# Sums carried on in the matmul banks in the seven-product jobs of a decoder block

## The chip, the cores and the metric

The kernel runs on one core of a Trainium2 chip. Its engines are named here as the profile names them: TensorE (PE) multiplies matrices into PSUM, which this kernel uses as eight banks of 128 partitions by 512 float32; VectorE (DVE) and ScalarE (ACT) do elementwise work and read and write PSUM and SBUF; GpSimd (POOL) and SyncE (SP) mostly issue transfers. The metric is the device time of one execution in microseconds (us); less is better.

## The reference

One layer of a decoder block, float32, 1024 tokens of 1024 features:

```python
proj = rms_norm(x) @ w_in       # stick-breaking q, k, v | gated-linear q, k, v, output gate r, code a | two gates
o_sb  = stick_breaking_attention(sb_q, sb_k, sb_v)                      # 8 heads of 64
log_a = log_sigmoid(g_a @ w_alpha_up + b_alpha) / 16
o_gla = norm_per_head(gla_chunked(g_q, g_k, g_v, log_a)) * gla_norm_g * silu(g_r)
y = sigmoid(gate_sb + b0) * (o_sb @ w_branch_sb) + sigmoid(gate_gla + b1) * (o_gla @ w_branch_gla)
h = x + y @ w_out
a, g = split(rms_norm(h) @ w_ffn_in)                                    # 2816 features each
h = h + (gelu(causal_conv3(a)) * g) @ w_ffn_out
return rms_norm(h)
```

The change lies in two of these products: a part of `@ w_in`, and `@ w_ffn_in`.

## The kernel before

**Precision.** Every operand is cut into a high and a low part: `split` lets ScalarE cast the high part (L119) and VectorE subtract it from the source for the low part (L110). A product over 512 contraction rows, `mac` (L195), is 4 contraction tiles by 3 matmuls (high by high, high by low, low by high), twelve matmuls of 128x128 by 128x512 into one bank.

**A job.** `fast` computes two blocks of 128 output features for all 1024 tokens at once. It treats them as a 2x2 block product and does it in seven products of quarters instead of eight (Strassen, in Winograd's form). The weight quarters b11, b12, b21, b22 of a job, and their sums s1 to s4, are cut by `piece` into w11, w1, w2, w3, w4, w21 and w22; the tokens' quarters 11, 12, 22 and their sums s1 to s4 lie ready in `q`. Each product gets a bank of its own, in the order w11, w2, w3, w4, w1, w21, w22. ScalarE copies the first into c (L280). VectorE then adds up (all L116): u = w2 + c, g = w3 + u, the upper half of o1 = w4 + g, g = w1 + g, u = w1 + u, the lower half of o1 = w21 + c, u = w22 + u. u and g are the two halves of o2. While a job's products run, the next job's weights are loaded (L171) and cut: `first_pieces` (w11, w2) behind the fourth product, `more_pieces` (w3, w4, w1) behind the last; w21 and w22 are cut in their own job.

**Where it runs.** Ten jobs are projections, `@ w_in` (from about 113 to 311 us in the trace): two for the gated-linear queries and keys, four for the stick-breaking ones, two for the output gate r, two for branch gates. Numbered 0 to 9, jobs 1, 3, 5 and 7 have steps of `decayed` between them and their forerunner: two matmuls on TensorE (L467) and, on ScalarE, L468, L469, L470 and L471, of which the last two load another table of functions first (ACT_TABLE_LOAD); L501 and L502 are the transposes of an earlier step and their copy. The output gates' jobs, 6 and 7, end with a sigmoid of 128x1024 on both results (L513), the branch gates' with L516. Twenty-two jobs are `@ w_ffn_in` (about 834 to 1230 us): each ends with the convolution `ff_out`, begun by ScalarE (L996), carried on by VectorE (L998 twice), then gelu (L1000) and a multiplication (L113). Six of the twenty-two have two of their products done earlier (`done` is set); sixteen have all seven in the job.

**Behind the projections** the attention begins: `qk` loads queries and keys of a pair of heads (L573, L574, L567, L571, SP's queue), casts them (L578, L581), subtracts (L110, 64x1024), and `weigh` multiplies them (L631, L632), with sigmoids L634 and L635 behind. Between them stand products of the remaining gates (`gates`, L195). Behind the feed-forward jobs stands the output stage (L1098).

**Order.** A scheduler puts each engine's instructions into one fixed order when the kernel is built; on the chip each engine runs its list in that order and waits where an operand or a buffer is not ready. SBUF tiles come from rings of 8, 4 and 2 KB (`t8`, `t4`, `t2`); a new tile waits for the last users of the slot it is given.

## Time and profile before

| what | value |
|---|---|
| time, median of 3 runs | 1451.14 us (1451.05 to 1451.71) |
| span of the profiled execution | 1448.6 us |
| TensorE busy | 1428.3 us (99%), 6569 matmuls |
| VectorE busy | 1102.5 us (76%) |
| ScalarE busy | 682.1 us (47%) |
| GpSimd busy | 152.9 us (11%) |
| matmuls of L195 | 3648, 869.8 us |
| share of L195 in the chain that ended last | 56% |

The span runs from the first to the last instruction of one profiled execution; the times of the runs are taken without the profile and hold some microseconds around it. Busy time is the sum of an engine's instructions. The chain that ended last is followed back from the last instruction, at each step to what released it.

### The profile page before, as it was taken

The page shows a single profiled execution, that of the slowest core. Times are in us where ns is not written, and L with a number is a line of the kernel's source. Part 1 is how long each engine was busy: PE and PEld are TensorE (multiplying, and loading weights), DVE is VectorE, ACT ScalarE, POOL GpSimd, SP SyncE. Part 2 cuts the span into 40 slices and gives each one's busy share as a digit, 9 for nine tenths or more (in the row PEclk, how much of TensorE's full clock was granted, in tenths as well). Part 3 has the DMA queues.
Part 4 walks back from the last instruction along what each step waited for, and adds up shares of the span by engine and source line. Part 5 has one row for each costly group of instructions (what it writes and reads, how often), then busy time and mean ns, then how long its engine had stood idle before and what let it go on. Part 6 is the DMA issues. An engine that isn't in the chain of part 4 may idle for free.

```text
span 1448.6 us, 18651 instructions
## 1 busy us (share of the span) xinstructions
PE 1428.3 (99%) x6569; PEld 1154.1 (80%) x6569; DVE 1102.5 (76%) x1737; ACT 682.1 (47%) x1310; POOL 152.9 (11%) x277
## 2 busy tenths in 40 slices
PE   7999999999999999999999999999999999999997
PEld 6788888877777778878888888888888888888886
DVE  6397667868988976735834999898888887897855
ACT  6225444647867665452322643343333333554554
POOL 0000000022442431300000000010000000000000
PEclk9999999999999999999999999999999999999999
DMA  6332342467525415637332622755534436963332
GB/s 243 127 107 73 109 123 89 138 218 206 129 77 138 124 47 174 215 104 243 125 131 87 175 73 93 242 177 179 168 126 162 164 116 232 339 199 102 96 102 102
DMA packets 156798, 212.67 MB, mean 147 GB/s; under 512 B 9713, under 2 KB 102963, under 8 KB 156192
## 3 DMA queue, kind: packets, MB, share of 16 engines
q1 hardware_dynamic: 138096, 155.44, 35.4%
q0 software_dynamic: 11312, 41.48, 7.5%
q10 hardware_dynamic: 7296, 14.55, 2.7%
q8 instruction: 52, 0.85, 0.2%
q14 instruction: 42, 0.34, 0.1%
HBM read 153.64 MB, written 57.80 MB: 146 GB/s over the span
## 4 chain that ended last, share of the span: by engine, by line
PE 94%; DVE 3%; DMA 1%; ACT 1%; issue 1%; SPq 0%; DVEq 0%; ACTq 0%
PE bank L195 56%; PE bank L1098 14%; PE bank L366 6%; PE bank L965 5%; PE bank L663 2%; PE bank L654 2%; PE bank L632 2%; DVE t L110 2%; PE bank L631 1%; PE bank L319 1%; PE bank L794 1%; PE bank L789 1%; DVE t L116 1%; PE bank L774 1%; DMA t<-sqk_d 1%
## 5 line engine op out<-in xcount | busy, mean ns | idle before, releaser
L195 PE MATMUL bank<-t,t 128*128 128x512 f32 x3648 | 869.8, 394 | 0.8 <-DVE t L110 0.8
L195 PEld LDWEIGHTS bank<-t,t 128*128 128x128 f32 x3648 | 677.5, 188 | 155.6 <-issue 10.2
L110 DVE TENSOR_TENSOR t<-t,t 128x512 fp32r<-128x512 f32 (+1 forms) x659 | 439.3, 699 | 90.5 <-ACT t L119 81.0
L119 ACT CAST t<-t 128x512 fp32r<-128x512 f32 x537 | 311.3, 619 | 296.2 <-DVE t L110 68.4
L116 DVE TENSOR_TENSOR t<-bank,t 128x512 f32<-128x512 f32 (+1 forms) x284 | 182.9, 654 | 116.5 <-PE bank L195 67.1
L1098 PE MATMUL bank<-t,t 128*128 128x512 f32 x924 | 209.6, 389 | 0.0
L1098 PEld LDWEIGHTS bank<-t,t 128*128 128x128 f32 x924 | 173.4, 188 | 36.0
L113 DVE TENSOR_TENSOR t<-t,t 128x511 f32<-128x511 f32 (+5 forms) x134 | 92.8, 697 | 2.1 <-ACT t L513 0.8
L366 PE MATMUL bank<-t,t 128*128 128x512 f32 x384 | 90.8, 395 | 0.0
L965 PE MATMUL bank<-t,t 128*128 128x512 f32 x384 | 88.9, 391 | 0.0
L110 DVE TENSOR_TENSOR t<-bank,t 128x512 fp32r<-128x512 f32 (+4 forms) x128 | 72.5, 576 | 19.7 <-ACT t L119 19.4
L996 ACT ACTIVATE t<-t,vcol 128x1024 f32<-128x1024 f32 x22 | 27.4, 1245 | 127.4 <-DVE t L116 127.4
L366 PEld LDWEIGHTS bank<-t,t 128*128 128x128 f32 x384 | 72.0, 189 | 15.4 <-DVE t L110 0.4
L965 PEld LDWEIGHTS bank<-t,t 128*128 128x128 f32 x384 | 71.7, 188 | 14.6
L116 DVE TENSOR_TENSOR t<-t,t 128x512 f32<-128x512 f32 x107 | 70.2, 687 | 16.1 <-ACT t L471 15.3
L110 DVE TENSOR_TENSOR t<-t 128x512 f32<-128x512 f32 x116 | 78.5, 685 | 4.1 <-DMA t<-in_w_ffn_in_dram 3.7
L119 ACT CAST t<-bank 128x512 fp32r<-128x512 f32 (+3 forms) x124 | 61.7, 512 | 38.6 <-PE bank L319 19.0
L638 POOL TENSOR_SCALAR_AFFINE_SELECT t<-t 128x128 f32<-128x128 f32 x128 | 66.2, 535 | 123.3 <-ACT t L634 118.2
L998 DVE SCALAR_TENSOR_TENSOR t<-t,vcol,t 128x1023 f32<-128x1023 f32 (+1 forms) x44 | 56.3, 1278 | 14.1 <-ACT t L996 13.9
L646 DVE TENSOR_TENSOR_SCAN t<-t,zero 128x128 f32<-128x128 f32 (+1 forms) x64 | 52.3, 821 | 15.9 <-POOL t L638 15.7
L634 ACT ACTIVATE t<-bank 128x128 f32<-128x128 f32 (+3 forms) x96 | 48.2, 502 | 17.2 <-PE bank L632 15.0
L654 PE MATMUL bank<-ident,t 128*128 128x128 f32 x288 | 49.7, 278 | 1.7 <-DVE t L113 0.9
(125 smaller groups left out, 891.1 us busy)
## 6 DMA issues: line engine op xcount, KB each, us to landing
t<-in_w_ffn_in_dram SPq DMA_DIRECT2D x50, 512.0 KB, 5.0
t<-in_w_in_dram SPq DMA_DIRECT2D x43, 512.0 KB, 5.3
act_d<-t POOLq DMA_DIRECT2D x22, 512.0 KB, 5.8
t<-in_w_ffn_out_dram SPq DMA_DIRECT2D x22, 512.0 KB, 6.5
wsum_d<-t POOLq DMA_DIRECT2D x22, 512.0 KB, 4.6
t<-act_d SPq DMA_DIRECT2D x22, 512.0 KB, 5.8
t<-wsum_d SPq DMA_DIRECT2D x44, 256.0 KB, 3.2
t<-sqk_d SPq DMA_DIRECT2D x40, 256.0 KB, 5.7
```

Of the source, the lines that this page charges most:

```text
L110: nc.vector.tensor_tensor(out=o, in0=a, in1=b, op=ALU.subtract)
L113: nc.vector.tensor_tensor(out=o, in0=a, in1=b, op=ALU.mult)
L116: nc.vector.tensor_tensor(out=o, in0=a, in1=b, op=ALU.add)
L119: nc.scalar.copy(h, src)
L195: nc.tensor.matmul(pt, a[:, kk], b[:, kk], start=start and kk == 0 and m == 0, stop=stop and kk == k - 1 and m == 2)
L366: nc.tensor.matmul(pt, a[:, k % 4, t], b, start=k == 0 and m == 0, stop=k == NK - 1 and m == 2)
L638: nc.gpsimd.affine_select(out=a[:, w - P:w], in_=a[:, w - P:w], pattern=[[-1, P]], compare_op=ALU.is_gt, fill=fill_, base=0, channel_multi ...
L646: nc.vector.tensor_tensor_scan(out=kr, data0=kr, data1=zero.to_broadcast([P, w]), initial=initial, op0=ALU.mult, op1=ALU.add)
L654: nc.tensor.transpose(pt[:, b * P:(b + 1) * P], be[:, b * P:(b + 1) * P], ident)
L965: nc.tensor.matmul(pt, a[:, k % 4, t], b, start=(k == 0 and m == 0), stop=(k == NK - 1 and m == 2))
L998: nc.vector.scalar_tensor_tensor(out=cv[:, i:], in0=av[:, :S - i], scalar=col(V_CW, (2 - i) * NF + f), in1=cv[:, i:], op0=ALU.mult, op1=AL ...
L1098: nc.tensor.matmul(pts[m][i], a[:, t], b, start=(k == 0 and x_ == 0), stop=(k == NH - 1 and x_ == 2))
```

## The change

Jobs whose seven products are all still to do (ten projections, sixteen of feed-forward) take a new function, `whole`. It uses three banks, px, py and pz. The products run in the order w11 (px), w1 (py), w2 (onto px), w21 (pz), w3 (onto px), w22 (onto py), w4 (onto px). `mac` gets a switch `more`, with which its first matmul does not clear the bank. ScalarE copies px after w11 (c), py after w1 (g), px after w2 (u) and px after w4 (the upper half of o1); VectorE adds the lower half of o1 = pz + c, g = px + g after w3, u = py + u after w22. For these jobs w1 is cut in `first_pieces`. The six jobs with `done` set keep the old way.

```diff
-    def mac(w, r, k=4, pt=None, start=True, stop=True):
+    def mac(w, r, k=4, pt=None, start=True, stop=True, more=False):
+        start = start and not more
...
                 nc.tensor.matmul(pt, a[:, kk], b[:, kk], start=start and kk == 0 and m == 0,
-                                 stop=stop and kk == k - 1 and m == 2)
+                                 stop=stop and kk == k - 1 and m == 2, skip_group_check=more)
...
             sub(s2, b22, r["s1"])
+            if r["done"] is None:
+                r["w1"] = piece(r["s1"])
             r["w2"] = piece(s2)
...
             r["w4"] = piece(s4)
-            r["w1"] = piece(r["s1"])
+            if r["done"] is not None:
+                r["w1"] = piece(r["s1"])
+
+        def whole(r, nxt, o1, u, g):
+            px, py, pz = bank(), bank(), bank()
+            c = t2()
+            mac(r["w11"], q["11"], pt=px)
+            nc.scalar.copy(c, px)
+            w21 = piece(r["a"][:, 4:])
+            mac(r["w1"], q["s1"], pt=py)
+            nc.scalar.copy(g, py)
+            w22 = piece(r["b"][:, 4:])
+            mac(r["w2"], q["s2"], pt=px, more=True)
+            nc.scalar.copy(u, px)
+            mac(w21, q["12"], pt=pz)
+            add(o1[:, :HALF], pz, c)
+            if nxt is not None:
+                first_pieces(nxt)
+            yield
+            mac(r["w3"], q["s3"], pt=px, more=True)
+            add(g, px, g)
+            mac(w22, q["s4"], pt=py, more=True)
+            add(u, py, u)
+            if nxt is not None:
+                more_pieces(nxt)
+            mac(r["w4"], q["22"], pt=px, more=True)
+            nc.scalar.copy(o1[:, HALF:], px)
...
             if r["done"] is None:
-                c = t2()
-                nc.scalar.copy(c, mac(r["w11"], q["11"]))
-            else:
-                c = r["done"][:, :HALF]
-                nc.scalar.copy(o1[:, :HALF], r["done"][:, HALF:])
+                yield from whole(r, nxt, o1, u, g)
+                finish(o1, o2)
+                yield
+                continue
+            c = r["done"][:, :HALF]
+            nc.scalar.copy(o1[:, :HALF], r["done"][:, HALF:])
...
-                    if r["done"] is None:
-                        w21 = piece(r["a"][:, 4:])
...
-            if r["done"] is None:
-                add(o1[:, :HALF], mac(w21, q["12"]), c)
```

The lines of the changed kernel are numbered anew. In the new `fast`, L260 is the copy c, L263 g, L266 u, L279 the upper half of o1, and L198 the matmul; of the lines behind it L497 to L500 are the decays' L468 to L471, L512 and L513 their L483 and L484, L531 and L532 the L502 and L503 of before, L542 the sigmoid of L513, L1025 and L1027 the convolution's L996 and L998, and L1127 the matmul of L1098.

Three places in the order of the engines follow. ScalarE between jobs 6 and 7, before: the sigmoids of job 6's two results (L513), between them the copy of the transposes (L502).

```order
L513 ACT_TABLE_LOAD
L513 ACTIVATE t4_329_2037<-t4_308_1906 128x1024
L502 COPY t2_280_1740<-bank_331_2045 128x512
L513 ACTIVATE t4_330_2041<-t4_309_1907 128x1024
L503 DMA kt_d_83<-t2_280_1740 128x512
```

And now, from the last copy of job 6 (L279) on:

```order
L279 COPY t4_284_1876<-bank_286_1878 128x512
L531 COPY t2_260_1715<-bank_303_2010 128x512
L542 ACT_TABLE_LOAD
L542 ACTIVATE t4_301_2002<-t4_284_1876 128x1024
L542 ACTIVATE t4_302_2006<-t4_285_1877 128x1024
```

Both sigmoids now stand behind the last copy of job 6.

A little later on ScalarE, in job 7, before: the two casts for w21 and w22 (L119), the last table load of the decays ahead of c, and the copy c (L280).

```order
L119 CAST t4_341_2088<-t8_307_1903 128x512
L471 ACT_TABLE_LOAD
L471 ACTIVATE t2_332_2052<-t2_332_2052 128x512
L119 CAST t4_342_2091<-t8_307_1903 128x512
L280 COPY t2_339_2073<-bank_340_2074 128x512
```

And now, to the copy c (L260):

```order
L119 CAST t4_315_2055<-t8_283_1873 128x512
L500 ACT_TABLE_LOAD
L500 ACTIVATE t2_304_2017<-t2_304_2017 128x512
L263 COPY t4_310_2037<-bank_312_2039 128x512
L119 CAST t4_316_2071<-t8_283_1873 128x512
L260 COPY t2_314_2041<-bank_311_2038 128x512
```

The copy of the second product (L263) now stands ahead of the copy c, beside the cast for w22.

TensorE in the same job, before: the end of the first product (bank_340) and the start of the second, in a bank of its own.

```order
L195 MATMUL bank_340_2074<-t8_3_97,t4_317_1971 128x512 x2
L195 MATMUL bank_340_2074<-t8_4_98,t4_317_1971 128x512
L195 MATMUL bank_340_2074<-t8_3_97,t4_317_1971 128x512
L195 MATMUL bank_343_2094<-t8_116_714,t4_320_1978 128x512
L195 MATMUL bank_343_2094<-t8_117_715,t4_320_1978 128x512
L195 MATMUL bank_343_2094<-t8_116_714,t4_320_1978 128x512 x2
```

And now: the end of w1's product (bank_312), eight matmuls of w21's (bank_313), and the start of w2's, which goes on in the first product's bank_311 and waits for the copy c.

```order
L198 MATMUL bank_312_2039<-t8_127_797,t4_295_1947 128x512
L198 MATMUL bank_312_2039<-t8_126_796,t4_295_1947 128x512
L198 MATMUL bank_313_2040<-t8_5_99,t4_315_2055 128x512
L198 MATMUL bank_313_2040<-t8_6_100,t4_315_2055 128x512
L198 MATMUL bank_313_2040<-t8_5_99,t4_315_2055 128x512 x2
L198 MATMUL bank_313_2040<-t8_6_100,t4_315_2055 128x512
L198 MATMUL bank_313_2040<-t8_5_99,t4_315_2055 128x512 x2
L198 MATMUL bank_313_2040<-t8_6_100,t4_315_2055 128x512
L198 MATMUL bank_311_2038<-t8_116_714,t4_296_1950 128x512
L198 MATMUL bank_311_2038<-t8_117_715,t4_296_1950 128x512
```

What was a product into a fresh bank is a product onto a bank that ScalarE reads first.

VectorE at the end of the last feed-forward job, before: from its last sums to the subtractions for the output stage (the low parts of t4_1949 to t4_1952 and t4_1909, t4_1910).

```order
L116 TENSOR_TENSOR t4_1922_10708<-bank_1932_10788,t2_1924_10710 128x512
L998 SCALAR_TENSOR_TENSOR t4_1934_10816<-t4_1922_10708,vcol_75,t4_1934_10816 128x1023
L116 TENSOR_TENSOR t4_1923_10709<-bank_1933_10802,t4_1923_10709 128x512
L998 SCALAR_TENSOR_TENSOR t4_1934_10816<-t4_1922_10708,vcol_75,t4_1934_10816 128x1022
L110 TENSOR_TENSOR t4_1949_10864<-t8_1946_10858,t4_1949_10864 128x512
L110 TENSOR_TENSOR t4_1950_10867<-t2_1947_10860,t4_1950_10867 128x512
L113 TENSOR_TENSOR t4_1934_10816<-t4_1934_10816,t4_1923_10709 128x1024
L110 TENSOR_TENSOR t8_1946_10858<-t8_1946_10858 128x512
L110 TENSOR_TENSOR t4_1909_10632<-t2_1955_10905,t4_1909_10632 128x512
L110 TENSOR_TENSOR t4_1910_10635<-t8_1959_10943,t4_1910_10635 128x512
L110 TENSOR_TENSOR t4_1951_10883<-t8_1946_10858,t4_1951_10883 128x512
L110 TENSOR_TENSOR t4_1952_10886<-t2_1948_10862,t4_1952_10886 128x512
```

And now (t4_1845 to t4_1848 take the place of t4_1949 to t4_1952):

```order
L116 TENSOR_TENSOR t4_1823_10584<-bank_1824_10585,t4_1823_10584 128x512
L116 TENSOR_TENSOR t4_1823_10584<-bank_1825_10586,t4_1823_10584 128x512
L1027 SCALAR_TENSOR_TENSOR t4_1830_10686<-t4_1822_10583,vcol_75,t4_1830_10686 128x1023
L110 TENSOR_TENSOR t4_1845_10734<-t8_1842_10728,t4_1845_10734 128x512
L1027 SCALAR_TENSOR_TENSOR t4_1830_10686<-t4_1822_10583,vcol_75,t4_1830_10686 128x1022
L110 TENSOR_TENSOR t4_1846_10737<-t2_1843_10730,t4_1846_10737 128x512
L110 TENSOR_TENSOR t8_1842_10728<-t8_1842_10728 128x512
L113 TENSOR_TENSOR t4_1830_10686<-t4_1830_10686,t4_1823_10584 128x1024
L110 TENSOR_TENSOR t4_1847_10753<-t8_1842_10728,t4_1847_10753 128x512
L110 TENSOR_TENSOR t4_1848_10756<-t2_1844_10732,t4_1848_10756 128x512
L110 TENSOR_TENSOR t4_1852_10777<-t8_1849_10771,t4_1852_10777 128x512
```

The convolution's steps (L1027) come behind all three sums, and its multiplication (L113) stands ahead of the subtractions for t4_1847 and t4_1848; two subtractions that stood ahead of their likes (t4_1909, t4_1910) are behind now.

## Rows read from the trace of the kernel before

**Rows 1.** The page, part 1: busy time of each engine, share of the span, instructions.

```profile
PE 1428.3 (99%) x6569; PEld 1154.1 (80%) x6569; DVE 1102.5 (76%) x1737; ACT 682.1 (47%) x1310; POOL 152.9 (11%) x277
```

**Rows 2.** The chain in order of time: start, duration (us), what, matmuls.

```profile
834.11 396.51 PE bank L195 x1748
1230.62 209.45 PE bank L1098 x924
```

**Rows 3.** Stretches: length; busy PE, PEld, DVE, ACT, POOL (count); clock, DMA share, GB/s.

```profile
312.00:372.00 60.00, 58.71 (x277) 43.51 (x278) 52.09 (x85) 46.80 (x96) 20.75 (x36) 1.00 0.64 185
...
1002.00:1230.00 228.00, 228.00 (x1007) 188.79 (x1006) 190.60 (x275) 80.23 (x121) 12.79 (x24) 1.00 0.48 159
```

**Rows 4.** Waits of PE: line, what it waited for, us, times, longest.

```profile
PE bank L319 <- DVE t L311: 9.2, 1, 9.2
```

**Rows 5.** Instructions by line and shape: busy us, mean ns; idle before them, what ended it.

```profile
L1000 ACT ACTIVATE t<-t 128x1024 f32<-128x1024 f32 x22 | 23.4, 1062 | 40.1 <-DVE t L998 40.1
...
L280 ACT COPY t<-bank 128x512 f32<-128x512 f32 x26 | 15.0, 576 | 31.6 <-PE bank L195 31.6
...
L471 ACT ACT_TABLE_LOAD x4 | 5.1, 1283 | 0.1
```

```profile
L116 DVE TENSOR_TENSOR t<-bank,t 128x512 f32<-128x512 f32 x252 | 170.1, 686 | 106.0 <-PE bank L195 67.1 <-PE bank L965 37.0 <-PE bank L1098 1.7
```

**Rows 6.** Timeline at the start of job 1: start, duration (us), engine, instruction [idle before].

```profile
133.65 11.63 PE L195 MATMUL bank<-t,t 128*128 128x512 f32 x50
...
138.82 0.57 ACT L280 COPY t<-bank 128x512 f32<-128x512 f32 x1
```

**Rows 7.** Timeline at the start of job 7.

```profile
251.47 0.60 PE L501 MATMUL bank<-ident,t 128*128 128x128 f32 x4
...
252.11 0.59 ACT L502 COPY t<-bank 128x512 f32<-128x512 f32 x1
...
252.59 1.06 ACT L513 ACTIVATE t<-t 128x1024 f32<-128x1024 f32 x1
...
253.05 10.27 PE L195 MATMUL bank<-t,t 128*128 128x512 f32 x44
253.55 0.68 ACT L468 ACTIVATE t<-bank,vcol 128x512 f32<-128x512 f32 x1
...
256.66 0.60 ACT L119 CAST t<-t 128x512 fp32r<-128x512 f32 x1
257.28 1.28 ACT L471 ACT_TABLE_LOAD   x1
...
258.58 0.63 ACT L471 ACTIVATE t<-t 128x512 f32<-128x512 f32 x1
259.11 0.60 ACT L119 CAST t<-t 128x512 fp32r<-128x512 f32 x1
...
259.62 0.58 ACT L280 COPY t<-bank 128x512 f32<-128x512 f32 x1
```

**Rows 8.** Timeline from the last projection job to the attention.

```profile
290.06 2.66 SPq L574 DMA_DIRECT2D t<-sqk_d  x4
...
291.27 0.60 PE L501 MATMUL bank<-ident,t 128*128 128x128 f32 x4
...
296.39 6.31 SPq L171 DMA_DIRECT2D t<-in_w_in_dram  x2
...
304.73 1.14 ACT L119 CAST t<-t 128x512 fp32r<-128x512 f32 x2 [5.30 <-DMA t<-in_w_in_dram]
...
306.17 4.85 DVE L110 TENSOR_TENSOR t<-t,t 64x1024 fp32r<-64x1024 f32 x4
...
310.80 0.22 PE L631 MATMUL bank<-t,t 128*128 128x128 f32 x1
```

**Rows 9.** Timeline at the end of the feed-forward jobs.

```profile
1228.66 1.25 ACT L996 ACTIVATE t<-t,vcol 128x1024 f32<-128x1024 f32 x1 [11.96 <-DVE t L116]
```

```profile
1235.95 3.69 DVE L110 TENSOR_TENSOR t<-t,t 128x512 fp32r<-128x512 f32 x6
```

## The prediction

> **What bounds the kernel now.** I read the share of busy time first: TensorE is busy 99% of the span, VectorE 76%, ScalarE 47% [rows 1]. So a microsecond taken from VectorE is worth nothing by itself; it counts only where TensorE waits for it. The chain in time says whether it does: one piece of 396.51 us holds 1748 matmuls of the products end to end, 0.2268 us each, and the next piece, 209.45 us with 924 matmuls of the output stage, has 0.2267 [rows 2]. A product of twelve matmuls is 12 x 0.2268 = 2.72 us, and there is no room between them. By stretch: in the 228 us of steady feed-forward jobs TensorE idles for nothing while VectorE works 190.60; in the 60 us behind the projections it loses 1.29 [rows 3]. Of all 1448.6 - 1428.3 = 20.3 us of TensorE idle time [rows 1], 9.2 are one wait at the start [rows 4] and 8.5 lie behind the last matmul (1448.6 - 1230.62 - 209.45) [rows 1, 2]. **Some 2.6 us are all that any relief inside could give back.** So the question is not what VectorE saves but whether the new waits of TensorE are hidden.
>
> **What leaves and what comes.** In each of the 26 changed jobs four VectorE adds go (7 to 3) and three ScalarE copies come (1 to 4). 26 x 4 x 0.686 = 71 us of VectorE and 26 x 3 x 0.576 = 45 us of ScalarE [rows 5]; both engines have idle time, so both count nothing on the path. The 84 matmuls of a job stay. Call the products in their new order P1 to P7 (P1 w11, P2 w1, P3 w2, P4 w21, P5 w3, P6 w22, P7 w4). P3, P5 and P7 add onto P1's bank, P6 onto P2's. An add onto a bank may start only when the partial sum in it has been read: P3 waits for the copy c behind P1, P5 for the copy u behind P3, P6 for the copy g behind P2, P7 for VectorE's add behind P5. Before, every product had a bank of its own, and nothing on TensorE waited for these readers. Behind such a wait the whole TensorE queue stands, since its order is fixed.
>
> **Steady feed-forward jobs (16): nothing.** Count T from the end of the job before. ScalarE first has the copy of that job's last sum (0.58), its convolution (1.25 [rows 9]), and one weight cast (0.60), so it is free at about 2.5; P1 ends at 2.72, so c ends at 3.4 against 5.44, when P2 ends. The u copy ends 0.65 behind P3 and has P4's 2.72 us; the add behind P5 (0.686) has P6's. The gelu (1.06 [rows 5]) falls between c and g, and g has until P5's end. The cover is each time one whole other product, and the least margin about 2.0 us. If an edge of 2 us were missed, every microsecond missed would count 16 times (a rival, below).
>
> Two things move besides. The weights of w1, needed second now, are cut one step earlier, a job ahead, by the same two ScalarE casts and subtractions. And a job's convolution needs the last product now, not the sixth, so it, the gelu and the store behind it come 2.6 us later in their job; what is stored is read back only in the output stage, many jobs later, so only the last job's matters (below).
>
> **Job 1, the first decays: 0.3 us.** ScalarE does the decays and two loads of its tables ahead of c. c's copy ran at 138.82 and ended at 139.39; P1 started at 133.65, and with P2 behind it TensorE will want c at 133.65 + 2 x 2.73 = 139.11 [rows 6]. Stall 0.3 (0 to 0.6). In jobs 3 and 5 one table load fewer (1.28 [rows 5]) stands ahead of c, so 1.0 us is left over; in the others without decays there is as much room as in the steady jobs.
>
> **Job 7, decays behind two silu gates: 2.9 us.** Here ScalarE must do job 6's two sigmoids as well. Let T be 251.47, where the transposes behind job 6 start [rows 7]. Before, the first sigmoid ran ahead of T, since its sum was ready early; now its half o1 is P7's and is copied only after T, so both sigmoids come after. The copy of the transposed block starts at T + 0.64 and hands over 0.5 later; then a table load (1.3), two sigmoids (1.0 each from start to start): the decays' first step starts at T + 4.45. From there the old rows give the pace: 253.55 to the second weight cast at 259.11 is 5.56, and 0.5 from there to c [rows 7]. In the new order two steps stand ahead of c at this place, g and a cast: 4.45 + 5.56 = 10.0 for g, 10.5 for the cast, 11.1 for c, which ends at 11.7. TensorE: P1 starts at T + 1.58, P2 ends at 7.04, and the order puts eight matmuls of P4 next, to 8.86 unless they wait themselves (their operand's cast ends at 4.45 + 3.11 + 0.6 = 8.2, within the same stall). Then P3: 11.7 - 8.86 = **2.9 us** (2.3 to 3.5). Before, c came at T + 8.73, and no one on TensorE waited for it. P5's copy u is ready at 15.0, with TensorE there at 15.3: no second stall. The 2.9 us cannot be caught up later, as everything behind is bound by TensorE.
>
> The table load lasts 1.28 us at 257.28, and the next step starts 1.30 behind its start [rows 7]. The Trainium skill, page ScalarE: Activation LUTs, section on what ACT_TABLE_LOAD costs, counts a drain of 1.38 us more for each switch; with three loads ahead of c that would make job 7's stall 7.0 us, with two job 1's 3.1, and the whole some 1462. The row shows no such drain, so it decides, and the rule gets no chance of its own.
>
> **The passage to the attention: 0.8 us.** The keys' loads were issued at 290.06, 1.2 us before the last projection job began (its transposes ran at 291.27) [rows 8]. They go into an SBUF slot. Now that slot is the one of s1's low part, read last by the second product of that job: free at T + 0.6 + 2 x 2.73 = T + 6.1, 7.3 us later than before. SP's queue is held up behind it: the rest of the keys, the queries' rests and the gates' weights. Before, the last were issued from 296.39 and cast from 304.73, 8.3 us later; the first attention matmul ran at 310.80, T + 19.5, right when the job was over [rows 8]. Now the issue of the weights begins at about T + 11.4 and their cast at 20, the third of the four subtractions (4.85 in all [rows 8]) ends at about 20.1 to 20.7, where the products are over at 19.8: 0.3 to 0.9. The gate's first matmul, reached at 21.1, finds its weights between 20.9 and 23.3. Together 0 to 2.5; I take 0.8, since the row with 8.3 us to the cast is the nearest.
>
> **The passage to the output stage: 0.2 us.** The last job's convolution began at 1228.66, 2.0 us before its products ended [rows 2, 9]; now it needs the last product, so it comes at T + 0.6. VectorE's subtractions for the next stage stand behind it: the fourth of the six from 1235.95 ended at T + 7.8 [rows 9]; in the new order two of those ahead are moved behind it, and it ends at 8.5. TensorE wants it at 36 to 38 matmuls, 8.2 to 8.6. 0 to 0.8; I take 0.2.
>
> **Sum.** 0.3 + 2.9 + 0.8 + 0.2 = +4.2 us. The profiled span is 1448.6 and the median 1451.14, 2.5 above it; the difference goes on the median: **1455.3 us**.
>
> **Rivals.**
> *No change.* Job 7's c copy comes earlier than my sum of starts says, or the passages cost nothing: 1451 to 1454.0. For it: margins of under 1 us in my working, and TensorE's long pieces, which show that this order was met everywhere [rows 2]. Against it: three of the four ends would all have to fall low. Chance 0.24.
> *Faster.* With 119 fewer waits on the product line TensorE loses less between matmuls, and the 2.6 us inside shrink. At most 1451.1 - 2.6 = 1448.5, a little lower if the start-up of products that follow VectorE closely gets shorter. Against it: in the steady jobs TensorE already runs at the pace of the waitless output stage, 0.2268 to 0.2267 [rows 2]. Chance 0.06.
> *A wait in every job.* The convolution starts late in the feed-forward jobs, c slips past P2's end, and P3 waits. It decides once ScalarE frees itself later than T + 4.8. At 0.5 us for each of 16 jobs: +8, so 1463. For it: VectorE, on which the gelu hangs, works 84% of these stretches [rows 3]. Against it: c stands ahead of the gelu on ScalarE. Chance 0.07.
> The Trainium skill, page Perfetto Trace Analysis, section Matmuls, says that independent groups of matmuls should rotate through PSUM banks, so that one bank is emptied while the next group runs. With no overlap at all the 78 copies would lie bare, 45 us, and the whole come to some 1496. In this kernel another bank's product lies between in every case, 2.72 us against 0.576 [rows 2, 5], so that end belongs to the chance above and gets next to nothing of it.
> *The clock falls.* A stall of 2.9 us leaves TensorE idle, and it goes on at 1.2 instead of 2.4 GHz; a product would take 5.4 us, some 3 to 5 us more: 1459. Against it: TensorE waited 9.2 us at the start [rows 4], and the granted clock of the two stretches with and without gaps is 1.00, the higher level [rows 3]. Chance 0.03.
> My forecast, stalls in a few places, 1454.0 to 1458, has 0.60.
>
> **How the numbers follow.** A difference of 0.2%, 2.9 us, is about what a measurement of this kernel can tell from no change, so "slower" begins at 1454.0. Slower: 0.60 + 0.07 + 0.03 = 0.70; the same 0.24; faster 0.06. The range takes the likeliest case with its bounds (2.3 + 0 to 3.5 + 0.6 + 2.5 + 0.8 = 7.4) and most of the "no change" case, down to 1451.5; the rest of the slower rivals is left out: 1451.5 to 1459.
>
> **What would show it.** Waits of TensorE on the product line: one of about 3 us in job 7 (near 260 us), released by ScalarE, c's line; one of 0.3 near 139; none in the steady jobs, whose chain should be one piece at 0.2268. The keys' loads issued about 7 us later relative to the last projection job, with a wait near 315. VectorE's busy time down by 71 us and ScalarE's up by 45. I am wrong if job 7's wait is under 2 us, if TensorE waits in steady jobs, or if a matmul's mean pace in the products changes at either level of the clock.

## The result, and the profile after

The changed kernel takes 1457.83 us (median, 1457.59 to 1459.01) against 1451.10 of the kernel before on the same chip: plus 6.7 us, a ratio of 1.0048 (95% interval 1.0035 to 1.0061). The forecast was 1455.3 in 1451.5 to 1459.0, slower. The direction and the range held; 2.5 us of the loss were missed.

The page of the kernel after, part 1, to be set beside [rows 1]:

```profile
PE 1431.5 (98%) x6569; PEld 1154.4 (79%) x6569; DVE 1039.5 (71%) x1633; ACT 718.5 (49%) x1388; POOL 149.6 (10%) x277
```

VectorE did lose 104 instructions and ScalarE gained 78, as counted. TensorE does the same 6569 matmuls. What it waits for has grown; the view of its waits (line, what it waited for, us, times, longest) is to be set beside [rows 4]:

```profile
PE bank L348 <- DVE t L340: 9.0, 1, 9.0
PE bank L198 <- ACT t L260: 3.0, 2, 1.9
PE bank L198 <- ACT t L119: 1.4, 2, 0.9
...
PE bank L198 <- DVE t L110: 0.8, 1, 0.8
...
PE bank L198 <- DVE t L116: 0.4, 1, 0.4
```

In the kernel before, the product line had one wait, that ahead of the first feed-forward job:

```profile
PE bank L195 <- DVE t L110: 0.8, 1, 0.8
```

The copy c (L260) is new among the releasers, twice, with 3.0 us. The chain in order of time shows where the feed-forward one falls; of the one piece of 1748 matmuls in [rows 2] these are left:

```profile
838.37 70.12 PE bank L198 x308
909.11 7.48 DMA t<-in_w_ffn_out_dram
949.19 288.66 PE bank L198 x1272
```

From 949.19 on, 1272 matmuls run end to end at 0.2269 us, the pace of before. Between the two pieces the chain leaves TensorE for a load of w_ffn_out and for VectorE. The stretches (columns as in [rows 3]) show the place, 930 to 945 us, and that the jobs behind it are whole:

```profile
930.00:945.00 15.00, 13.06 (x58) 10.47 (x57) 15.00 (x23) 8.13 (x14) 1.59 (x3) 1.00 0.55 208
```

```profile
1010.00:1238.00 228.00, 228.00 (x1008) 188.79 (x1007) 161.98 (x226) 97.19 (x155) 12.76 (x24) 1.00 0.51 161
```

**Where the time went, stage by stage.** For every kernel I read eight marks from TensorE's timeline and its chain: the first matmul of the projections (113.62 in the kernel before), the transposes ahead of jobs 3, 7 and 9 (171.86, 251.47, 291.27), the first 24 gate matmuls in a row behind the first attention matmuls (321.16), the first feed-forward job behind its wait for VectorE (834.11), and the first and last matmul of the output stage. Lengths between marks, less those of the kernel before, in us; "elsewhere" is the rest of the span: the start, the attention and the store at the end. These differ by about 1 us from one execution to another even where the instructions are the same (the attention of ffn_only has the instructions of before in the same order and took 1.0 us longer). "Timed" is the difference of the medians. "Sum" and "elsewhere" come from one traced execution, "timed" from all: the trace of the changed kernel is that of its slowest execution, 1459.01 us.

| kernel | job 1 | jobs 7, 8 | to the attention | feed-forward | output stage | sum | elsewhere | timed |
|---|---|---|---|---|---|---|---|---|
| forecast | 0.3 | 2.9 | 0.8 | 0 | 0.2 | 4.2 | | |
| changed kernel | 0.34 | 2.92 | 0.51 | 2.97 | 0.40 | 7.1 | 1.5 | 6.7 |
| ffn_only | 0 | 0 | 0 | 2.12 | 0.37 | 2.5 | 1.2 | 3.4 |
| proj_only | 0.35 | 2.89 | 0.51 | 0.02 | 0 | 3.8 | 1.3 | 4.5 |
| tail_only | 0 | 0 | 0 | 0.01 | 0.37 | 0.4 | 0.1 | 0.4 |
| tail_copies6 | 0 | 0 | 0 | 5.10 | 0.35 | 5.5 | -0.4 | 5.5 |
| job6_old | 0.35 | 0.51 | 0.50 | 3.88 | 0.37 | 5.6 | 0.4 | 4.5 |
| three_old | 0 | 2.16 | 0.50 | 1.41 | 0.36 | 4.4 | 0.5 | 7.6 |
| from_26 | 0.35 | 2.91 | 0.51 | 0.00 | 4.55 | 8.3 | 0.2 | 8.3 |
| sums_later | 0.35 | 2.88 | 0.51 | 3.96 | 0.38 | 8.1 | 0 | 6.9 |
| no_sum_work | 0.34 | 2.92 | 0.50 | 7.62 | 0.40 | 11.8 | 0.5 | 11.9 |
| order_only | 0 | 0.41 | 0.50 | 0.28 | 0.25 | 1.4 | 0.8 | 4.2 |
| order_later | 0 | 0.43 | 2.71 | 0.14 | 0.27 | 3.6 | 1.7 | 2.4 |
| late_later | 0.25 | 1.78 | 0.49 | 2.49 | 0.25 | 5.3 | 1.5 | 6.0 |

Four of my five terms came out within 0.3 us, and they repeat in the kernels that keep the code in question; from_26 adds a loss of its own in the output stage. The feed-forward term is the one that failed.

### The profile page after: what moved, and what is told of

Read it like the earlier page. It is cut to its first block, busy times and chain, and to the rows that moved or that the text cites. A ratio compares the mean times of both kernels' runs of the same rounds, so it can differ in the third digit from the quotient of the medians.

```text
span 1457.2 us, 18493 instructions
## 1 busy us (share of the span) xinstructions
PE 1431.5 (98%) x6569; PEld 1154.4 (79%) x6569; DVE 1039.5 (71%) x1633; ACT 718.5 (49%) x1388; POOL 149.6 (10%) x277
## 4 chain that ended last, share of the span: by engine, by line
PE 90%; DVE 4%; ACT 2%; DMA 2%; issue 1%; SPq 0%; DVEq 0%; ACTq 0%
PE bank L198 52%; PE bank L1127 14%; PE bank L395 6%; PE bank L994 5%; DVE t L110 3%; PE bank L692 2%; PE bank L683 2%; PE bank L661 2%; PE bank L660 1%; DVE t L116 1%; PE bank L823 1%; PE bank L348 1%; PE bank L818 1%; PE bank L803 1%; DMA t<-sqk_d 1%
## 5 line engine op out<-in xcount | busy, mean ns | idle before, releaser
L198 PE MATMUL bank<-t,t 128*128 128x512 f32 x3648 | 872.0, 394 | 5.6 <-ACT t L260 3.0
L198 PEld LDWEIGHTS bank<-t,t 128*128 128x128 f32 x3648 | 677.0, 188 | 162.9 <-issue 9.4
L119 ACT CAST t<-t 128x512 fp32r<-128x512 f32 x537 | 308.0, 620 | 215.9 <-PE bank L1127 54.0
L1127 PE MATMUL bank<-t,t 128*128 128x512 f32 x924 | 210.0, 389 | 0.0
L1127 PEld LDWEIGHTS bank<-t,t 128*128 128x128 f32 x924 | 173.3, 188 | 36.6 <-DVE t L110 0.6
L116 DVE TENSOR_TENSOR t<-bank,t 128x512 f32<-128x512 f32 (+1 forms) x180 | 113.7, 635 | 109.3 <-PE bank L198 59.4
L113 DVE TENSOR_TENSOR t<-t,t 128x511 f32<-128x511 f32 (+5 forms) x134 | 92.5, 695 | 11.2 <-ACT t L542 9.2
L279 ACT COPY t<-bank 128x512 f32<-128x512 f32 x26 | 15.3, 587 | 171.3 <-PE bank L198 171.3
L1027 DVE SCALAR_TENSOR_TENSOR t<-t,vcol,t 128x1023 f32<-128x1023 f32 (+1 forms) x44 | 56.3, 1279 | 42.9 <-ACT t L1025 42.7
L119 ACT CAST t<-bank 128x512 fp32r<-128x512 f32 (+3 forms) x124 | 61.8, 513 | 38.6 <-PE bank L348 19.5
```

The lines of the kernel that those rows point to most:

```text
L113: nc.vector.tensor_tensor(out=o, in0=a, in1=b, op=ALU.mult)
L116: nc.vector.tensor_tensor(out=o, in0=a, in1=b, op=ALU.add)
L119: nc.scalar.copy(h, src)
L198: nc.tensor.matmul(pt, a[:, kk], b[:, kk], start=start and kk == 0 and m == 0, stop=stop and kk == k - 1 and m == 2, skip_group_check=more)
L1027: nc.vector.scalar_tensor_tensor(out=cv[:, i:], in0=av[:, :S - i], scalar=col(V_CW, (2 - i) * NF + f), in1=cv[:, i:], op0=ALU.mult, op1=AL ...
L1127: nc.tensor.matmul(pts[m][i], a[:, t], b, start=(k == 0 and x_ == 0), stop=(k == NH - 1 and x_ == 2))
```

## The experiments

**Which jobs.** A parameter of `fast` names the jobs that keep the form of before. It serves six of the runs, each with its own two lists, projections and feed-forward:

```diff
-    def fast(jobs, q, early=0):
+    def fast(jobs, q, early=0, old=()):
...
-                return dict(zip("ab", load_pair(*jobs[n][0])), done=ahead.popleft() if ahead else None)
+                r = dict(zip("ab", load_pair(*jobs[n][0])), done=ahead.popleft() if ahead else None)
+                r["carry"] = r["done"] is None and n not in old
+                return r
...
-            if r["done"] is None:
+            if r["carry"]:
                 yield from whole(r, nxt, o1, u, g)
```

The old form stands behind it as it was, and w1 is cut early only where `carry` is set.

*ffn_only* (projections: all old; feed-forward: none).

> Only the sixteen feed-forward jobs use the new form; the ten projection jobs are as before. Theory (the loss sits at a few named places: job 1 0.3 us, job 7 2.9, passage to the attention 0.5, first feed-forward job with all seven products 2.9, passage to the output stage 0.4): before plus 3.3, some 1454.4 us, with TensorE waits of 1.9 and 0.4 us near 932 and 944 us and none between 113 and 312. Rival (every job of the new form loses a little, 6.7 / 26 = 0.26 us): plus 4.1, some 1455.2, with no wait above 0.5 us.

1453.99 against 1450.63 us, ratio 1.0023 (1.0014 to 1.0032). In the trace 2.12 + 0.37 us, with TensorE's wait for c of 1.1 us at 933 us and one of 0.39 for VectorE's sum at 945, and nothing in the fifteen jobs behind.

*proj_only* (projections: none; feed-forward: all old).

> Only the ten projection jobs use the new form. Theory (named places): plus 0.3 + 2.9 + 0.5 = 3.7, some 1454.8 us, and the feed-forward stage as long as before (396.5 us in one piece). Rival (every job loses 0.26 us): plus 2.6, some 1453.7.

1455.16 us, ratio 1.0032 (1.0019 to 1.0044). The three terms of the projections repeat to 0.03 us, and the feed-forward stage is one piece of 396.52 us again. So the loss sits in places; but the two runs don't tell yet whether the steady jobs are free.

*tail_only* (projections: all old; feed-forward: the first ten old, so the new form is in the last twelve).

> The new form only in the last twelve feed-forward jobs, where VectorE has room; all else as before. Theory (steady jobs of the new form cost nothing, the passage to the output stage 0.4): 1451.2 + 0.4, some 1451.6 us, the same as before within 0.1%. Rival (each job of the new form loses 0.26 us by its waits): 12 x 0.26 = 3.1, some 1454.3.

1451.24 against 1450.86 us, ratio 1.0003 (0.9993 to 1.0012). Twelve jobs of the new form cost 0.01 us in their stage and 0.37 in the output stage. The rival of 0.26 us a job is out. The view of TensorE's waits has one on the product line, that ahead of the first feed-forward job, and none for a copy:

```profile
...
PE bank L198 <- DVE t L110: 0.8, 1, 0.8
```

The Trainium skill, page Perfetto Trace Analysis, section Matmuls, would have independent groups rotate through different banks, so that emptying one overlaps the next group's matmuls. The changed jobs carry one sum on in a bank instead, and here one other product between two on the same bank was enough in all twelve jobs. tail_only is also the answer to what the change could give: 48 VectorE sums fewer, and no time.

*tail_copies6*: the same, with the copy c made six times over.

```diff
-            nc.scalar.copy(c, px)
+            for _ in range(6):
+                nc.scalar.copy(c, px)
```

> As the run before it, but the copy c is made six times over in each of the twelve jobs (five further ScalarE copies of 0.58 us, 0.52 from start to start). Theory (c has 2.0 us to spare, and no more): the four copies that stand ahead of the gelu end at 4.9 us of the job, the sixth, behind gelu and g, at about 7.9; TensorE, which here takes some nine matmuls of the fourth product ahead, wants the bank at about 7.6: 0.3 to 0.5 us lost in each job, 4 to 6 in all, with TensorE waiting for c's line. Rival (ScalarE's copies are hidden however many, or the margin is larger): as the run before it.

1456.34 us, 5.1 above tail_only, ratio to before 1.0038 (1.0023 to 1.0052); in the trace 5.10 us in twelve jobs, 0.42 each, where 0.3 to 0.5 was worked out from the margin of 2.0 us. The timeline of one job (start, duration, engine, instruction [idle before it, and what ended that]) shows four copies, the gelu, the fifth, g, the sixth, and the wait at TensorE's weight load:

```profile
1063.71 2.45 ACT L261 COPY t<-bank 128x512 f32<-128x512 f32 x4 [0.35 <-PE bank L198]
1066.05 1.06 ACT L1040 ACTIVATE t<-t 128x1024 f32<-128x1024 f32 x1
1067.02 0.57 ACT L261 COPY t<-bank 128x512 f32<-128x512 f32 x1
1067.48 0.60 ACT L264 COPY t<-bank 128x512 f32<-128x512 f32 x1
1067.95 0.61 ACT L261 COPY t<-bank 128x512 f32<-128x512 f32 x1
...
1068.62 1.46 PEld L198 LDWEIGHTS bank<-t,t 128*128 128x128 f32 x7 [0.38 <-ACT t L261]
```

So in a steady job the copy is hidden as the hand-made timeline has it, and the cover is finite: the wait is there to be found as soon as ScalarE comes later than that.

**Job 7.** *job6_old* (projections: job 6 old; feed-forward: none).

> The changed kernel, but projection job 6 (the silu gates ahead of job 7) in the form of before, so that its first sigmoid can run ahead of job 7 again, while job 7 keeps its copy c and two table loads. Theory (job 7's wait is c standing behind two sigmoids that came late): the waits in job 7 fall from 2.9 to 0.5 us in all, 1455.4 us. Rival (the decays' table loads alone make it): it stays at 2.9, 1457.8.

1455.74 us, ratio 1.0031 (1.0020 to 1.0042). Jobs 7 and 8 lose 0.51 us instead of 2.92, as expected; the two table loads are the same. Here ScalarE's first sigmoid runs at 250.06, ahead of the transposes at 251.86, and c ends 9.2 behind these; the rows answer to [rows 7]:

```profile
250.06 1.06 ACT L552 ACTIVATE t<-t 128x1024 f32<-128x1024 f32 x1 [6.96 <-DVE t L116]
...
253.94 0.68 ACT L507 ACTIVATE t<-bank,vcol 128x512 f32<-128x512 f32 x1
...
260.49 0.59 ACT L260 COPY t<-bank 128x512 f32<-128x512 f32 x1
```

In the changed kernel the sigmoids come behind the last copy, both together, and c ends 11.6 behind the transposes (252.46):

```profile
252.66 0.58 ACT L279 COPY t<-bank 128x512 f32<-128x512 f32 x1 [7.70 <-PE bank L198]
...
255.04 2.01 ACT L542 ACTIVATE t<-t 128x1024 f32<-128x1024 f32 x2
...
256.96 0.67 ACT L497 ACTIVATE t<-bank,vcol 128x512 f32<-128x512 f32 x1
...
260.71 2.37 PE L198 MATMUL bank<-t,t 128*128 128x512 f32 x8 [0.94 <-ACT t L119]
...
263.49 0.59 ACT L260 COPY t<-bank 128x512 f32<-128x512 f32 x1
...
264.13 4.22 PE L198 MATMUL bank<-t,t 128*128 128x512 f32 x17 [1.05 <-ACT t L260]
```

I had put c's end at T + 11.7 and the decays' first step at T + 4.45; they were at 11.6 and 4.5. Both of TensorE's waits that the text named are there, for the cast of w21 and for c; 0.94 + 1.05, and the rest of the 2.92 lies inside the pieces (eight matmuls in 2.37 us, where 1.8 do). The wait itself was shared: c's line released only 1.05 us of it.

*three_old* (projections: jobs 1 and 7 old; feed-forward: the first with seven products old).

> The new form everywhere but in projection jobs 1 and 7 and in the first feed-forward job with all seven products, which keep the form of before. Theory (named places): 0.5 + 0.4 are left, some 1452.0 us. Rival (every job loses 0.26 us): 23 x 0.26 = 5.9, some 1457.0. Second rival (the feed-forward wait belongs to whichever job comes first in the new form, behind one of the old form): it turns up one job later, plus 3.8, some 1454.9.

1458.18 us (1455.29 to 1458.99), ratio 1.0047 (1.0034 to 1.0059): neither 1452 nor 1457 by its reasons. Job 1's term is gone. Job 7's is not; it moved to job 8, whose c now stands behind job 7's two sigmoids and two table loads, in ScalarE's timeline

```profile
273.75 1.28 ACT L552 ACT_TABLE_LOAD   x1
275.04 2.01 ACT L552 ACTIVATE t<-t 128x1024 f32<-128x1024 f32 x2
277.07 1.28 ACT L526 ACT_TABLE_LOAD   x1
...
278.90 0.57 ACT L260 COPY t<-bank 128x512 f32<-128x512 f32 x1
```

with a TensorE wait of 1.88 us. The feed-forward wait moved too, two jobs on, and shows its cause better than before (next). The median is 3 us above the traced execution, which was the fastest (1455.29). Its granted clock over the whole span was 0.998, that of the four other runs 0.996 or 0.997; 0.001 to 0.002 of 1455 us is some 1.5 to 3 us (an estimate), so TensorE at its lower clock is the likeliest place of the difference. Where in those runs it fell, one trace can't say.

**The feed-forward wait.** In the changed kernel it stands at the first job of the new form. TensorE wanted c at 935.68 and got it 1.94 us later; ScalarE had waited for VectorE with a cast, then did the convolution, a cast, and c:

```profile
934.81 0.62 ACT L119 CAST t<-t 128x512 fp32r<-128x512 f32 x1 [1.72 <-DVE t L110]
...
935.34 1.24 ACT L1025 ACTIVATE t<-t,vcol 128x1024 f32<-128x1024 f32 x1
936.48 0.60 ACT L119 CAST t<-t 128x512 fp32r<-128x512 f32 x1
...
936.99 0.57 ACT L260 COPY t<-bank 128x512 f32<-128x512 f32 x1
...
937.62 11.17 PE L198 MATMUL bank<-t,t 128*128 128x512 f32 x48 [1.94 <-ACT t L260]
```

VectorE is busy without a pause there (15.00 of 15 us in the stretch above). In the kernel before it was too, and c came equally late: it ended at 933.1, where the new order would have wanted it at 834.11 + 428 x 0.2268 = 931.2, 1.9 us earlier, as in the changed kernel (937.56 against 935.68). These rows of the kernel before, which I had not read, say so, and TensorE goes on at 100% beside them:

```profile
932.52 0.58 ACT L280 COPY t<-bank 128x512 f32<-128x512 f32 x1
```

```profile
915.00:930.00 15.00, 15.00 (x68) 12.43 (x67) 15.00 (x23) 5.96 (x10) 1.60 (x3) 1.00 0.61 209
930.00:945.00 15.00, 15.00 (x68) 12.43 (x67) 15.00 (x23) 5.96 (x10) 0.53 (x1) 1.00 0.50 152
```

The work that fills VectorE here beside the jobs is the sums of w_ffn_out (`weight_sums`, a step every half job from here on), whose first step also waits for its load, in the changed kernel:

```profile
916.69 2.50 DVE L110 TENSOR_TENSOR t<-t,t 128x512 f32<-128x512 f32 x4 [4.76 <-DMA t<-in_w_ffn_out_dram]
```

*sums_later*: one empty step ahead of the first subtraction.

```diff
             b11, b12, b21, b22 = a[:, :HALF], a[:, HALF:], b[:, :HALF], b[:, HALF:]
             yield
+            if k == 0:
+                yield
```

> The changed kernel, with one empty step between the first load of the weight sums (w_ffn_out) and their first subtraction on VectorE, which waited 4.8 us there at 911 us; nothing else is changed. Theory (TensorE's waits at the first feed-forward job of the new form come from that wait, passed on through VectorE's sums, ScalarE's cast and convolution to the copy c): the 1.9 and 0.4 us waits near 937 and 949 are gone, 1457.8 - 2.9 = 1454.9 us, and the runs lie closer together. Rival (the first job behind the old form waits whatever VectorE does): as the changed kernel, 1457 to 1458.

1458.14 us, ratio 1.0045 (1.0032 to 1.0058). The stage loses 3.96 us, but this doesn't settle it: VectorE still waits 3.8 us for the load at 911 us, since the scheduler placed the step hardly later, and 1.75 us for another at 950. The edit did not take away what it was to take away. It moved the loss: c came in time here (it ended at 933.6, and TensorE wanted it at 837.8 + 428 x 0.2268 = 934.9), and TensorE waited 1.99 us for a sum by VectorE at 948 instead, with the clock at the lower level behind it (last section).

*no_sum_work*: the four VectorE instructions of each step left out.

```diff
             yield
-            sub(b22, b22, b12)
-            sub(b12, b12, b11)
             yield
-            add(b11, b22, b11)
-            sub(b21, b11, b21)
```

> The changed kernel without the four VectorE subtractions and additions in each step of the sums of w_ffn_out (the rows are loaded and stored as they are, so the output stage works on other numbers); the wait for their first load goes with them. Theory (the 3 us at the first feed-forward jobs of the new form come from a VectorE that is full there, 92% busy from 834 to 1002 us, so that sums and casts that c stands behind come late): TensorE waits for nothing between 840 and 1230 us, the stage takes 396.3 us. Rival (the first job of the new form behind the old form waits in any case): the wait of 1 to 2 us near 935 stays.

1462.7 us (one run, so without an interval): against the expectation, a wait of 5.0 us for c, until 939.56. Without these instructions the scheduler put c behind the gelu in this job, and the gelu waited 3.94 us for VectorE's convolution steps. It is the rival "a wait in every job" of the prediction, at one job: c behind the gelu, and then late.

```profile
937.98 1.06 ACT L1035 ACTIVATE t<-t 128x1024 f32<-128x1024 f32 x1 [3.94 <-DVE t L1033]
938.94 0.57 ACT L260 COPY t<-bank 128x512 f32<-128x512 f32 x1
...
939.56 5.79 PE L198 MATMUL bank<-t,t 128*128 128x512 f32 x14 [4.98 <-ACT t L260]
```

The edit leaves the loads and stores of the sums in place, and they hold up the same jobs: a weight cast on ScalarE waits 6.55 us for a store, as it does in the changed kernel (6.68) and in the kernel before (6.99), and VectorE waits 4.84 us behind that cast. So the run does not separate the arithmetic of the sums from their transfers.

```profile
916.22 0.62 ACT L119 CAST t<-t 128x512 fp32r<-128x512 f32 x1 [6.55 <-DMA act_d<-t]
```

*from_26*: the steps of the sums begin eight half jobs later.

```diff
-FFN_FROM = 18
+FFN_FROM = 26
```

> The changed kernel with the weight sums' steps begun eight half jobs later (FFN_FROM 26 for 18), so that the first jobs of the new form run while VectorE has no such work. Theory (VectorE full at that place): no wait at the first job of the new form; later, with three sums a job instead of seven, VectorE has room (in the changed kernel 162 of 228 us from 1010 us on), so at most 1 us: 1457.8 - 2 to 3 = 1455 to 1456. Rival (the wait belongs to the first job of the new form): 1457 to 1458 with the wait near 935.

The feed-forward stage takes as long as in the kernel before, in one piece, though its first job of the new form follows one of the old form as ever: the rival is out, and the wait belongs to the sums that run beside these jobs, by their arithmetic or by their transfers, which moved together. The order of c and gelu alone does not make it: c stands behind the gelu in this job here too, ended at 934.1, and TensorE wanted it at 838.07 + 428 x 0.2268 = 935.1.

```profile
838.07 396.51 PE L198 MATMUL bank<-t,t 128*128 128x512 f32 x1748 [0.77 <-DVE t L110]
```

The time is 1459.16 us all the same, ratio 1.0060 (1.0046 to 1.0073): the last steps now fall into the output stage, where VectorE waits for their load and TensorE for VectorE, 2.29 us of the 4.55 lost there; most of the rest is the lower clock behind that wait (last section).

```profile
1247.21 201.35 PE L1137 MATMUL bank<-t,t 128*128 128x512 f32 x880 [2.29 <-DVE t L110]
```

three_old shows how the load of w_ffn_out can reach TensorE, there at the third job with seven products. VectorE waits 4.84 us for w_ffn_out; the convolution stands behind that, the gelu waits for it 6.06 us, g, a cast and u stand behind the gelu, and TensorE waits for u:

```profile
969.30 0.69 DVE L110 TENSOR_TENSOR t<-t,t 128x512 f32<-128x512 f32 x1 [4.84 <-DMA t<-in_w_ffn_out_dram]
...
973.89 1.27 DVE L1037 SCALAR_TENSOR_TENSOR t<-t,vcol,t 128x1022 f32<-128x1022 f32 x1
...
975.26 1.06 ACT L1039 ACTIVATE t<-t 128x1024 f32<-128x1024 f32 x1 [6.06 <-DVE t L1037]
976.22 0.57 ACT L263 COPY t<-bank 128x512 f32<-128x512 f32 x1
...
977.21 0.59 ACT L266 COPY t<-bank 128x512 f32<-128x512 f32 x1
...
977.85 1.43 PE L198 MATMUL bank<-t,t 128*128 128x512 f32 x5 [1.11 <-ACT t L266]
```

**The carry or the order.** *order_only*: the new order of products and the early cut of w1, but a bank for each product.

```diff
-            px, py, pz = bank(), bank(), bank()
             c = t2()
-            mac(r["w11"], q["11"], pt=px)
-            nc.scalar.copy(c, px)
+            nc.scalar.copy(c, mac(r["w11"], q["11"]))
...
-            mac(r["w2"], q["s2"], pt=px, more=True)
-            nc.scalar.copy(u, px)
-            mac(w21, q["12"], pt=pz)
-            add(o1[:, :HALF], pz, c)
+            add(u, mac(r["w2"], q["s2"]), c)
+            add(o1[:, :HALF], mac(w21, q["12"]), c)
+            add(c, mac(r["w3"], q["s3"]), u)
+            add(u, py, u)
...
+            add(g, c, g)
+            add(u, mac(w22, q["s4"]), u)
...
+            add(o1[:, HALF:], mac(r["w4"], q["22"]), c)
```

(c holds the sum of w11, w2 and w3 by then.)

> The new order of the products and the early cut of w1, with the copies c and g, but every product in a bank of its own again and six sums by VectorE: no matmul waits for a reader of its bank. Theory (the waits for readers make the loss): within 1 us of before, 1450.5 to 1452.0. Rival (the order, with w21 and w1 needed earlier, or the earlier cut of w1 on ScalarE and VectorE makes it): plus 4 to 7, 1455 to 1458.

1454.80 us (1452.54 to 1457.08), ratio 1.0031 (1.0019 to 1.0043); but the trace, with a span of 1450.8 us that of the fastest execution (1452.54), shows only 1.4 us in the stages: 0.41 at jobs 7 and 8, the 0.50 at the passage to the attention, 0.28 and 0.25. So at the passage to the attention the loss is the order's and not the carry's, and job 1's and most of job 7's are the carry's. How much of the feed-forward term the order alone makes stays open: the other runs lie up to 4.5 us above this one.

*order_later*: the empty step of sums_later in this kernel.

> The same empty step in the kernel that has the new order with a bank for every product (order_only, 1454.8 us, its runs spread over 4.5 us). Theory (its loss is the same late load, which reaches TensorE through the cast of w21, needed fourth instead of sixth, with some 0.2 us to spare in the trace): 1451 to 1452, spread under 2 us. Rival (the order loses elsewhere): 1454 to 1455.

1453.58 us (1452.73 to 1456.45), ratio 1.0019 (1.0009 to 1.0028), between the two expectations, and the spread shrank little, from 4.5 to 3.7 us; as in sums_later the edit left the wait for the load (3.5 us). In this trace the passage to the attention took 2.71 instead of 0.50 us: TensorE's first attention matmul waits 0.5 us, the first gate matmul 0.41, and behind them, from 316 to 319, the granted clock was 0.50. Inconclusive for the load.

*late_later*: the carry begins with w2's product, and c is added by VectorE, so nothing on TensorE waits for ScalarE (with the same empty step).

```diff
-            mac(r["w11"], q["11"], pt=px)
-            nc.scalar.copy(c, px)
+            nc.scalar.copy(c, mac(r["w11"], q["11"]))
...
-            nc.scalar.copy(g, py)
+            add(g, py, c)
...
-            mac(r["w2"], q["s2"], pt=px, more=True)
-            nc.scalar.copy(u, px)
+            mac(r["w2"], q["s2"], pt=pw)
+            add(u, pw, c)
...
-            nc.scalar.copy(o1[:, HALF:], px)
+            add(o1[:, HALF:], pw, c)
```

> The same empty step, and the carried bank begins with w2's product instead of w11's: c is added by VectorE (to the second, the third, the fourth and the last product), so that no matmul waits for a ScalarE copy; the fifth waits for VectorE's sum behind the third. Six sums by VectorE, one copy by ScalarE. Theory (job 7's 2.9 us are the wait for c alone): no wait above 0.5 us in job 7, the passages' 0.5 and 0.4 are left, 1451.5 to 1452.5. Rival (any carry costs, by the wait of the next product for a reader): 1454 to 1457.

1457.21 us, ratio 1.0042 (1.0028 to 1.0055): the rival. Job 7 still loses 1.78 us, now in waits of 0.20 and 1.00 for VectorE, and the feed-forward stage 2.49, with one of 1.90 for VectorE's sum. Taking c off TensorE's list put VectorE's sum, which itself needs c, in its place.

No version beat the kernel before; tail_only, the one with the least loss, is equal to it within its interval.

## Why the prediction was right, and where it wasn't

- **The bound.** TensorE at 99% [rows 1] and products end to end [rows 2]: nothing was to be gained, and nothing was. tail_only shows it directly: 48 sums fewer, and 0.4 us slower, which its interval doesn't tell from no change.
- **Job 1, 0.3 us:** 0.34. c ended 5.73 us behind the job's first matmul (134.29 to 140.02), as the rows of before had it (5.74) [rows 6].
- **Job 7, 2.9 us:** 2.92, with the steps at the times that were added up from [rows 7], and job6_old shows that it was the sigmoids' place. The table load at 258.22 lasted 1.28 us and the next step began 1.30 behind its start. The drain that the Trainium skill, page ScalarE: Activation LUTs, section on what ACT_TABLE_LOAD costs, adds to each switch showed nowhere in this row; with the page's figure for three loads the term would, as an estimate, have been 4.1 us too high. The sign of being wrong that I had given for this term, a wait under 2 us in job 7, came true by a hair, with 0.94 + 1.05 = 1.99 us of waits, though the term held: a part of the loss does not show as a wait.
- **The passage to the attention, 0.8 us:** 0.51, and the reason is as told: the keys' loads were issued at 301.08, 5.9 us behind the last job's transposes (295.18), where they had been 1.2 us ahead of them [rows 8]. The subtractions came just in time, the first attention matmul 19.5 us behind those transposes as before, and the gate's weights were cast 20.4 behind them, so that TensorE waited 0.42 us for the cast. order_only has the same 0.50.
- **The passage to the output stage, 0.2 us:** 0.40, and 0.35 to 0.40 in the other kernels with the whole new form in the last job, from_26 apart, whose sums run into this stage. Mis-sized by 0.2.
- **"Steady feed-forward jobs (16): nothing."** Wrong for the first of them, right for those behind: 2.97 us, in the trace two waits of 1.94 (for c) and 0.40 us (for VectorE's sum) and some 0.6 us in the pieces behind them. I worked out one job from the middle of the stage and took it for all sixteen. In the first ones VectorE has no pause, with the sums of w_ffn_out beside them, and c, with ScalarE's casts ahead of it waiting for VectorE, came at the same time relative to the products as in the kernel before, where nothing waited for it. from_26 shows that the wait goes with the sums; whether by their arithmetic on VectorE or by their loads and stores stays open. The trace of before held the late c, as shown above. TensorE's waits in these jobs were another sign of being wrong in the prediction, and by it this part of the mechanism failed. What I had called the point from which the rival "a wait in every job" decides, ScalarE free later than T + 4.8, was reached in one job of sixteen.
- **The range, in part by luck.** Its upper end, 7.4 us, was made of upper bounds that the terms did not reach: 2.5 us of it was for the passage to the attention, which took 0.51. The 3 us of the feed-forward jobs, which the sum had at nothing, filled that slack.
- **Busy times.** I gave 71 us less and 45 more; the page shows 63.0 and 36.4, for the 104 and 78 instructions that were counted. An instruction's duration overlaps the next by some 0.1 us (0.686 long, 0.60 from start to start), and busy time counts that once.
- **Faster, and the falling clock:** neither happened in this kernel's trace; in the stretch with the longest new wait the granted clock stayed at 1.00 (930 to 945, above). But my argument against the falling clock did not bear on it: the two stretches of [rows 3] don't hold the wait of 9.2 us. Right behind that wait eight transposes (L319) took 1.94 us in the kernel before, and eight later ones, at 25.41 us, took 0.87. In variants with waits of about the same length the clock did fall (last section).

## What to carry to other kernels

Before a result of one engine is put between two steps of the engine that bounds the kernel, list when that result came in every repetition of the loop in the old trace, the first and last ones and those beside other work above all, not in a typical one: a copy that nobody waited for may have been late all along. When each product has a bank of its own, that lateness is free; carried sums make it a wait. And on this kernel, whose TensorE is at 99%, moving sums off VectorE was worth nothing by itself.

## What the runs showed of the hardware

In no_sum_work TensorE's clock fell: over the 5 us that hold most of its wait of 4.98 us for c the granted clock was 0.78, and over the next 5 us 0.54 of full speed, so mostly at the lower level, 1.2 GHz, and 14 matmuls took 5.79 us, 0.41 each instead of 0.227. In the changed kernel it stayed at 1.00 behind a wait of 1.94 us (930 to 945 us, above). The stretches of no_sum_work:

```profile
935.00:940.00 5.00, 0.44 (x1) 0.44 (x2) 4.42 (x6) 2.02 (x4) 0.00 (x0) 0.78 0.36 142
940.00:945.00 5.00, 5.00 (x14) 3.86 (x14) 2.70 (x5) 0.58 (x2) 0.53 (x1) 0.54 0.44 158
```

That is 5.79 - 14 x 0.227 = 2.6 us beyond the wait itself, and the two make the 7.62 us that this stage lost.

It fell behind shorter waits too, in runs whose losses stand in the table above: behind 1.98 us for c in job6_old, 1.99 us for VectorE's sum in sums_later and 2.29 us in from_26, where the granted clock was 0.50 from 1248 to 1250. The wait and the stretch, first of job6_old, then of sums_later (with TensorE's columns alone):

```profile
934.04 78.28 PE L198 MATMUL bank<-t,t 128*128 128x512 f32 x337 [1.98 <-ACT t L260]
930.00:940.00 10.00, 8.02 (x29) 0.83 0.38 134
```

```profile
948.04 64.23 PE L198 MATMUL bank<-t,t 128*128 128x512 f32 x275 [1.99 <-DVE t L116]
940.00:950.00 10.00, 8.01 (x32) 0.91 0.90 283
```

At 0.2268 us each, 337 matmuls take 76.4 us and 275 take 62.4, so some 1.9 us were lost behind each wait; wait and loss together make, within 0.1, the 3.88 and 3.96 us of these stages, and 2.29 + 201.35 - 880 x 0.2267 = 4.1 us of from_26's 4.55. Waits of nearly the same length, 1.94 us in the changed kernel and 1.98 in job6_old, went either way, so a wait's length alone did not tell whether the clock would fall. In the prediction I had given the falling clock 3 to 5 us behind job 7's wait; at that place the trace shows no fall. The price where it came was 1.9 to 2.6 us.
